# Conformer convolution in a two-layer trunk kernel: taps loaded and multiplied during the first FFN, second half of channels transformed in quarters, output projection by token tile

## The chip, the core and the metric

The kernel runs on one core of a Trainium2 chip. The metric is the device time of one execution, in microseconds. A core has five engines that run their own instruction queues: PE (TensorE, matrix products, with weight loads PEld), DVE (VectorE), ACT (ScalarE), POOL (GpSimd) and SP (SyncE, which here issues nearly all DMAs). They wait for each other through semaphores.

## What is computed

A backbone of two layers over 512 latent tokens of width 1024, with 256 context tokens; every sub-layer is wrapped in RMSNorm, a shift and scale from the conditioning vector, and a gated residual. Layer 0 mixes with a hybrid of gated DeltaNet heads and attention heads, layer 1 with a Conformer convolution; both end in a SwiGLU FFN. The change is in the Conformer:

```
def conformer_conv(h, w_in, b_in, dw_w, dw_b, ln_g, ln_b, w_out, b_out):
    val, gate = jnp.split(h @ w_in + b_in, 2, axis=-1)
    u = val * jax.nn.sigmoid(gate)
    u = depthwise_conv_centred(u, dw_w) + dw_b
    u = jax.nn.silu(layer_norm(u, ln_g, ln_b))
    return u @ w_out + b_out
```

`dw_w` has 31 taps for each of the 1024 channels. All data is fp32.

## The kernel before

**Products.** Each fp32 operand is split into a high part and a low part (a cast, then a subtraction), and each product is three matmuls: high by high, high by low, low by high. Weights come as 128x1024 tiles of 512 KB (`wraw`, L1700), are cast on ACT or DVE into `whi` (L564) and subtracted on DVE or POOL into `wlo` (L573). L564 and L573 are helpers for all casts and copies and all two-operand operations, so a group is told by its tiles.

**Order of work.** The program is written as operations with engines they may run on, a cost on each, what they depend on and which buffers they take and give back. The class `Plan` (from L62) sorts them: at every step it takes the operation with the earliest planned start, less a weight times the length of the work behind it and a bias from a table by the operation's name (`BIAS2`, L136, for this part). Buffers are counted as slots: 8 PSUM banks (`ps`), 46 slabs of 128x512 (`s`), 4 pairs of converted weights (`w`), 2 raw weight tiles (`wraw`), 2 window places (`win`). The result is a fixed order on every engine. `plan_tail` (from L1683) plans the last of four stretches: the output projection of the hybrid (phase 0), ffn(0) together with the dot products for later gates (phase 1), the Conformer (phase 2), ffn(1) (phase 3). The three stretches ahead of it are not touched.

**FFN.** For each pair of token tiles and each hidden slice, a gate bank and an up bank `ps_in` take 24 matmuls each (L204 to L206). ACT does silu from the gate bank (L1963), DVE multiplies with the up bank (L1966); only then are the banks free. The output projection (L1758 to L1760, `ps_y`) has two halves n of 512 columns and four token tiles t, a bank each. Each tile is squared and summed on ACT (L1779), multiplied by the gate row on DVE (`yg`, L1783), and added to the residual.

**Conformer.** The 1024 channels are worked in two halves n of 512. The input projection runs in four quarters q: n is q // 2, and each quarter brings 256 value and 256 gate columns for four token tiles (`ps_in`, L2105 to L2112). ACT takes the sigmoid of the gate (L2128), DVE multiplies (`csg`, L2131), and the result is split into `uh` and `ul`. The convolution is done by Fourier transform over the tokens. Three overlapping windows w cover two neighbouring token tiles each. `window(n, w)` makes real and imaginary parts with 12 matmuls into two banks `ps_ft` (L2166 to L2168), four products with the taps' spectra `specr` and `speci` on DVE (L2175), a sum and a difference, and two splits into `sph` and `spl`. `back(n, t)` transforms back into a bank `ps_y` (L2223 to L2229), one window for the outer token tiles, two for the inner ones. The bank is copied to `xtok` on ACT and its statistics are taken on DVE (`bs`, L2241). When both halves of a token tile are there, mean and variance are joined (L2266), POOL takes the root (L180), DVE normalises the two halves in place (`xtok`, L2278), PE transposes them (`ps_a`, L1830), ACT does silu with gain and bias (L2285), and the result is split into `ah` and `al` for the output projection, whose weights are `wcout`.

**The taps.** `ld_s` loads the taps in two halves (`taps`, L2065) and their 31 rows of cosines and sines (`tapf`, L2066), `s_mm` makes the spectra with four matmul groups into four banks `ps_sp` (L2076), and `s_put` copies these to `specr` and `speci`, which belong to buffers that open when ffn(0) has given up its own (`opened`).

## Time and profile before

| | us |
|---|---|
| median of 3 runs | 1390.94 (1390.02 to 1392.03) |
| the profiled execution | 1390.09 |
| its span | 1388.3 |
| PE busy | 1335.3 |
| DVE busy | 847.8 |
| ACT busy | 484.3 |
| POOL busy | 229.2 |

The profile is one execution; its times count from the start of the span. The page gives busy times, 40 slices with the clock that PE was granted, the chain of work that ended last, and groups of instructions by line, engine, operation and tile, with their mean time and what ended the idle time before them. Other views of the trace are the waits (which instruction waited for which engine's instruction, in total, how often, and the longest), the windows (busy time, count of instructions, clock and DMA share in a stretch) and the timeline. A matmul's own time overlaps that of its neighbours, so what one costs in a row of them is the stretch divided by their number.

### The profile page before, as it was taken

The numbers are of one execution on the slowest core, as the hardware profiler recorded it, in microseconds if no ns is written. First come the engines' busy times: TensorE is split into PE (matmuls) and PEld (weight loads), VectorE is DVE, ScalarE is ACT, GpSimd is POOL, SyncE is SP. The second block draws the span as 40 slices with busy tenths as digits, with TensorE's granted clock in tenths as the row PEclk, the third lists the DMA queues.
The fourth block names the chain that finished last, engine by engine and source line by source line (L and its number), as shares of the span: only waits on it lengthen the run. The fifth ranks groups of instructions, "written<-read, shape, count | busy, mean of one in ns | idle before, by whom it ended". The sixth has DMA issues, their size and how long they took to land.

```text
span 1388.3 us, 19096 instructions
## 1 busy us (share of the span) xinstructions
PE 1335.3 (96%) x7267; PEld 1121.0 (81%) x7267; DVE 847.8 (61%) x1631; ACT 484.3 (35%) x1019; POOL 229.2 (17%) x299
## 2 busy tenths in 40 slices
PE   6999998999999999999999899997999999999998
PEld 4888887889978988888888678885898888888886
DVE  3588897899877755656578454649464334343223
ACT  5656535776634211111100153214343222122221
POOL 2668562111002000000000210314040000000000
PEclk8999998999999999999999999998999999999999
DMA  8445635652265456455488413110213233233231
GB/s 313 139 131 172 149 121 117 208 160 89 65 198 196 145 160 197 153 165 182 163 269 270 160 48 105 61 46 31 76 62 122 78 104 103 79 122 106 91 101 66
DMA packets 105851, 184.74 MB, mean 133 GB/s; under 512 B 33731, under 2 KB 50450, under 8 KB 105760
## 3 DMA queue, kind: packets, MB, share of 16 engines
q1 hardware_dynamic: 105760, 183.53, 41.4%
q8 instruction: 57, 0.93, 0.3%
q14 instruction: 34, 0.28, 0.1%
HBM read 172.44 MB, written 11.06 MB: 132 GB/s over the span
## 4 chain that ended last, share of the span: by engine, by line
PE 82%; DVE 8%; DMA 4%; POOL 2%; ACT 2%; issue 1%; SPq 1%; DVEq 0%; POOLq 0%; ACTq 0%
PE ps_in L204 12%; PE ps_in L206 12%; PE ps_in L205 12%; PE ps_y L1758 7%; PE ps_y L1759 7%; PE ps_y L1760 7%; PE ps_in L2112 2%; PE ps_in L2110 2%; PE ps_in L2111 2%; PE ps_pt L1306 1%; PE ps_pv L1328 1%; PE ps_o L1369 1%; PE ps_sc L1276 1%; PE ps_du L1369 1%; PE ps_a L1830 1%
## 5 line engine op out<-in xcount | busy, mean ns | idle before, releaser
L206 PE MATMUL ps_in<-ah,wlo 128*128 128x512 f32 (+1 forms) x768 | 285.6, 372 | 1.1 <-DVE wlo L573 1.0
L204 PE MATMUL ps_in<-ah,whi 128*128 128x512 f32 (+1 forms) x768 | 285.7, 372 | 0.0
L205 PE MATMUL ps_in<-al,whi 128*128 128x512 f32 (+1 forms) x768 | 285.3, 371 | 0.0
L573 DVE TENSOR_TENSOR wlo<-wraw,whi 128x1024 fp32r<-128x1024 f32 x165 | 204.9, 1250 | 129.1 <-ACT whi L564 123.4
L206 PEld LDWEIGHTS ps_in<-ah,wlo 128*128 128x128 f32 x768 | 144.6, 188 | 26.7 <-DVE wlo L573 1.8
L204 PEld LDWEIGHTS ps_in<-ah,whi 128*128 128x128 f32 x768 | 144.7, 188 | 25.2 <-DVE whi L564 0.2
L205 PEld LDWEIGHTS ps_in<-al,whi 128*128 128x128 f32 x768 | 144.7, 188 | 24.9
L564 ACT CAST whi<-wraw 128x1024 fp32r<-128x1024 f32 x92 | 96.3, 1050 | 165.2 <-PE ps_y L1759 80.7
L1758 PE MATMUL ps_y<-whi,hh 128*128 128x512 f32 x352 | 138.9, 394 | 0.0
L1759 PE MATMUL ps_y<-whi,hl 128*128 128x512 f32 x352 | 138.4, 393 | 0.0
L1760 PE MATMUL ps_y<-wlo,hh 128*128 128x512 f32 x352 | 138.4, 393 | 0.0
L564 DVE CAST whi<-wraw 128x1024 fp32r<-128x1024 f32 x70 | 48.5, 693 | 140.7 <-PE ps_in L205 107.7
L1963 ACT ACTIVATE sg<-ps_in 128x512 f32<-128x512 f32 x44 | 26.3, 598 | 291.5 <-PE ps_in L206 291.2
L1625 DVE CUSTOM_DVE_ANT_0 wada<-wada,csrow 128x1024 f32<-128x1024 f32 x80 | 96.7, 1222 | 12.4 <-DMA wada<-in_wmB 12.0
L180 POOL TENSOR_TENSOR rr<-rr,mhalf 128x1 f32<-128x1 f32 x28 | 16.1, 576 | 489.5 <-DVE rr L1797 457.7
L1758 PEld LDWEIGHTS ps_y<-whi,hh 128*128 128x128 f32 x352 | 66.7, 189 | 15.9 <-issue 1.5
L1760 PEld LDWEIGHTS ps_y<-wlo,hh 128*128 128x128 f32 x352 | 66.6, 189 | 14.6
L1759 PEld LDWEIGHTS ps_y<-whi,hl 128*128 128x128 f32 x352 | 66.6, 189 | 14.4
L1966 DVE TENSOR_TENSOR sg<-sg,ps_in 128x512 f32<-128x512 f32 x44 | 30.0, 684 | 64.9 <-PE ps_in L206 64.9
L1779 ACT ACTIVATE junk<-ps_y 128x512 bf16<-128x512 f32 x32 | 19.1, 598 | 122.6 <-PE ps_y L1760 110.8
L573 POOL TENSOR_TENSOR matsl<-fraw,matsh 128x512 fp32r<-128x512 f32 x5 | 8.1, 1655 | 322.8 <-ACT matsh L564 322.8
L2110 PE MATMUL ps_in<-whi,ah 128*128 128x512 f32 x128 | 50.0, 391 | 0.0
(383 smaller groups left out, 2603.9 us busy)
## 6 DMA issues: line engine op xcount, KB each, us to landing
wraw<-in_wfin SPq DMA_DIRECT2D x88, 512.0 KB
wada<-in_wmB SPq DMA_DIRECT2D x80, 512.0 KB
wraw<-in_wfout SPq DMA_DIRECT2D x44, 512.0 KB
mraw<-in_wmA SPq DMA_DIRECT2D x16, 512.0 KB
wraw<-in_wcin SPq DMA_DIRECT2D x16, 512.0 KB
wraw<-in_wqkv SPq DMA_DIRECT2D x12, 512.0 KB
wraw<-in_wcout SPq DMA_DIRECT2D x8, 512.0 KB
rw<-grow SPq DMA_DIRECT2D x8, 384.0 KB
```

Source lines behind the costliest of these rows:

```text
L204: E.matmul(ps, wh, xh, start=start, stop=False)
L205: E.matmul(ps, wh, xl, start=False, stop=False)
L206: E.matmul(ps, wl, xh, start=False, stop=stop)
L564: {"ACT": S.copy, "DVE": V.tensor_copy, "Pool": G.tensor_copy}[e](dst, src)
L573: {"DVE": V, "Pool": G}[e].tensor_tensor(dst, a, b, o)
L1369: E.matmul(s[key][:m, h, 0:n], lhs(h), rhs(h), start=True, stop=True)
L1625: V.tensor_tensor_reduce(s["raw"], s["raw"], csrow[0], 1.0, 0.0, ALU.mult, ALU.add, accs[:, part, j : j + 1])
L1758: E.matmul(acc[t], ah[:, ts_], wh[:, o], start=i == 0 and j == 0, stop=False)
L1759: E.matmul(acc[t], al[:, ts_], wh[:, o], start=False, stop=False)
L1760: E.matmul(acc[t], ah[:, ts_], wl[:, o], start=False, stop=end)
L1966: V.tensor_tensor(s["g"], s["g"], pss[1]["ps"], ALU.mult)
L2110: E.matmul(acc[t], k["h"][:, tk], wh[:, o], start=False, stop=False)
```

## The change

Five edits, all in the tail or in the host's layout of the taps:

- The taps get a 32nd row of zeros, as do the cosines and sines; the three DMAs and the four matmul groups work on 32 rows. `ld_s` no longer depends on `opened`. `s_put` still does.
- The second half of channels is transformed in quarters of 256: `window_half(1, c, w)` takes the columns of quarter c alone, with 12 matmuls of 256 columns into one bank, which holds the real part in its left half and the imaginary part in its right. Its spectrum products are one of 512 and two of 256 columns, then one sum, one cast and one subtraction.
- `back(1, t)` runs in two passes of 256 columns into one bank.
- A window waits for the splits of its own quarter (`ops[c]`), where it waited for the last split of the half.
- The output projection of the Conformer takes its first half token tile by token tile, as the last four weight tiles of the second half already were (`bytile`).

The bias table `BIAS2` is new throughout. The diff, cut to its core:

```
-        def out_proj(lhs, src, part, ready, extra=None, free=None):
+        def out_proj(lhs, src, part, ready, extra=None, free=None, bytile=False):
...
-                by_i = np_ - 4 if n else np_
+                by_i = np_ - 4 if n or bytile else np_
...
-                    SP.dma_start(st["taps"][n][:31, :], I["cdw"][:, n * 512 : n * 512 + 512])
-                SP.dma_start(st["tapf"][:31, :256], I["ctap"])
-
-            ts_ = op({"SP": 3 * DMA}, ld_s, (opened,), lat=DLAT, take=("s", "s", "s"))
+                    SP.dma_start(st["taps"][n][:32, :], I["cdw"][:, n * 512 : n * 512 + 512])
+                SP.dma_start(st["tapf"][:32, :256], I["ctap"])
+
+            ts_ = op({"SP": 3 * DMA}, ld_s, lat=DLAT, take=("s", "s", "s"))
...
-                    ut["op"] = op({"DVE": 0.34, "Pool": 0.7}, c_low, (b,), rel=("s",))
+                    ut.setdefault("ops", []).append(op({"DVE": 0.34, "Pool": 0.7}, c_low, (b,), rel=("s",)))
...
+            def window_half(n, c, w):
...
+                def dft_q():
+                    s["ps"] = pbank("ps_ft")
+                    for i in range(2):
+                        o = s["ps"][:, i * 256 : i * 256 + 256]
+                        for j, (t, m) in enumerate(FWD[w]):
+                            mh, ml = mat(m + i)
+                            x = u[n][t]
+                            E.matmul(o, mh, x["h"][:, cc], start=j == 0, stop=False)
+                            E.matmul(o, mh, x["l"][:, cc], start=False, stop=False)
+                            E.matmul(o, ml, x["h"][:, cc], start=False, stop=j == 1)
...
+                def q_prod():
+                    s["x"] = slab("spa")
+                    V.tensor_tensor(s["x"].rearrange("p (i c) -> p i c", i=2), s["ps"].rearrange("p (i c) -> p i c", i=2),
+                                    bc(st["spec"][0][:, cs_], 1, (P, 2, 256)), ALU.mult)
...
+                def q_cross():
+                    s["y"] = slab("spb")
+                    V.tensor_tensor(s["y"][:, lo], s["ps"][:, hi], st["spec"][1][:, cs_], ALU.mult)
+                    V.scalar_tensor_tensor(s["y"][:, hi], s["ps"][:, lo], -1.0, st["spec"][1][:, cs_], op0=ALU.mult, op1=ALU.mult)
...
+                def q_comb():
+                    V.tensor_tensor(s["x"], s["x"], s["y"], ALU.add)
...
+                need = [u[n][t]["ops"][c] for t, _ in FWD[w]] + [mats[j] for j in range(2)]
...
+                for c in ((None,) if n == 0 else (0, 1)):
+                    cs_ = slice(0, 512) if c is None else slice(c * 256, c * 256 + 256)
...
+            for w in range(3):
+                window(0, w)
+            for w in range(3):
+                window_half(1, 0, w)
...
+            for t in range(NT):
+                back(0, t)
...
+            for w in range(3):
+                window_half(1, 1, w)
...
+            for t in range(NT):
+                back(1, t)
...
-            e = out_proj(lhs, I["wcout"], 6, ready, extra, free)
+            e = out_proj(lhs, I["wcout"], 6, ready, extra, free, True)
```

How the order moves, at three places. First SP's queue of DMAs, before, in ffn(0)'s output projection: `in_wfout` are its last weights, `in_wcin` the Conformer's first ones, `in_cmat` the transform matrices, `taps` and `tapf` the convolution's taps.

```order
L1700 DMA wraw<-in_wfout 128x1024
L2046 DMA fraw<-in_cmat 128x512 x5
L1700 DMA wraw<-in_wfout 128x1024
L2015 DMA bo<-in_cbias 8x512 x2
L1700 DMA wraw<-in_wcin 128x1024
L2065 DMA taps<-in_cdw 31x512 x2
L2066 DMA tapf<-in_ctap 31x256
L1700 DMA wraw<-in_wcin 128x1024
```

The same queue after, where the taps now stand, at the end of the hybrid's output projection: `in_wfin` are ffn(0)'s first weights, `in_wmB` the weights of the gates' dot products, `in_xs` the residual.

```order
L2390 DMA hres_5136<-in_xs 128x1024
L1622 DMA wada<-in_wmB 128x2x512 x3
L1700 DMA wraw<-in_wfin 128x1024 x4
L2065 DMA taps<-in_cdw 32x512 x2
L2066 DMA tapf<-in_ctap 32x256
L1622 DMA wada<-in_wmB 128x2x512 x4
```

The three transfers have moved from behind the first Conformer weight to a place ahead of nearly all of ffn(0)'s weights.

Second, PE before, in the second half of ffn(0)'s output projection (`ps_y`), around the four tap groups `ps_sp`:

```order
L1759 MATMUL ps_y<-whi,hl 128x512
L1760 MATMUL ps_y<-wlo,hh 128x512
L2076 MATMUL ps_sp<-taps,tapf 128x512 x4
L1758 MATMUL ps_y<-whi,hh 128x512
L1759 MATMUL ps_y<-whi,hl 128x512
```

PE after, in ffn(0)'s first hidden slices, which are worked 256 tokens wide:

```order
L206 MATMUL ps_in<-ah,wlo 128x256
L2076 MATMUL ps_sp<-taps,tapf 128x512
L204 MATMUL ps_in<-ah,whi 128x256
L205 MATMUL ps_in<-al,whi 128x256
L206 MATMUL ps_in<-ah,wlo 128x256
L204 MATMUL ps_in<-ah,whi 128x256
L205 MATMUL ps_in<-al,whi 128x256
L206 MATMUL ps_in<-ah,wlo 128x256
L2076 MATMUL ps_sp<-taps,tapf 128x512
```

The tap groups now stand one by one between ffn(0)'s matmuls, and nothing stands between the `ps_y` groups where they were.

Third, DVE before, where the last windows of the second half (`spa` to `spd`, `sph`, `spl`) meet the first normalisations (L2278):

```order
L564 CAST sph<-spa 128x512
L573 TENSOR_TENSOR spl<-spa,sph 128x512
L564 CAST sph<-spb 128x512
L573 TENSOR_TENSOR spl<-spb,sph 128x512
L2175 TENSOR_TENSOR spa<-ps_ft,specr 128x512
L2175 TENSOR_TENSOR spc<-ps_ft,speci 128x512
L2175 TENSOR_TENSOR spd<-ps_ft,speci 128x512
L2175 TENSOR_TENSOR spb<-ps_ft,specr 128x512
L2278 TENSOR_SCALAR xtok<-xtok,mv 128x512 x2
L564 CAST sph<-spa 128x512
L573 TENSOR_TENSOR spl<-spa,sph 128x512
```

DVE after, at its first normalisations (now L2348), with `csg` and `uh` of the last input tile between them:

```order
L573 TENSOR_TENSOR spl<-spa,sph 128x512
L2301 BN_STATS bs<-ps_y 128x6
L2336 BN_AGGR mv<-bs 128x2
L2337 TENSOR_SCALAR mv<-mv 128x1
L2348 TENSOR_SCALAR xtok<-xtok,mv 128x512 x2
L2131 TENSOR_TENSOR csg<-ps_in,csg 128x256
L564 CAST uh<-csg 128x256
L2348 TENSOR_SCALAR xtok<-xtok,mv 128x512 x2
L573 TENSOR_TENSOR wlo<-wraw,whi 128x1024
```

The four full-width products ahead of the first normalisation and the two splits behind it have gone; one quarter of the last window (`spa`, `spb` from L2237 on) stands after both pairs of normalisations.

More of the change, by code (lines that the diff above doesn't have):

```diff
@@ L2075, in s_mm @@
                         w["ps"] = pbank("ps_sp")
-                        E.matmul(w["ps"], st["tapf"][:31, i * P : i * P + P], st["taps"][n][:31, :], start=True, stop=True)
+                        E.matmul(w["ps"], st["tapf"][:32, i * P : i * P + P], st["taps"][n][:32, :], start=True, stop=True)
                     def s_put(e, n=n, i=i, w=w):
@@ L2197, in sp_lo @@
                     return f
-                need = [u[n][t]["op"] for t, _ in FWD[w]] + [mats[j] for j in range(2)]
+                need = [o for t, _ in FWD[w] for o in u[n][t]["ops"]] + [mats[j] for j in range(2)]
                 r = op({"PE": 1.36}, dft(0), need, take=("ps", "win"))
@@ L2215, in window, with q_hi, q_lo @@
                 s["used"] = []
[L2217 to L2233 removed]
+            def window_half(n, c, w):
+                s = ab[n, c, w] = {}
+                cc, cs_ = slice(c * 256, c * 256 + 256), slice(n * 512 + c * 256, n * 512 + c * 256 + 256)
+                lo, hi = slice(0, 256), slice(256, 512)
+                def dft_q():
[18 more added lines that the diff above has]
+                    V.tensor_tensor(s["x"], s["x"], s["y"], ALU.add)
+                def q_hi(e):
+                    s["h"] = slab("sph", F32R)
+                    copy_on(e, s["h"], s["x"])
+                def q_lo(e):
+                    s["l"] = slab("spl", F32R)
+                    tt_on(e, s["l"], s["x"], f32(s["h"]), ALU.subtract)
+                need = [u[n][t]["ops"][c] for t, _ in FWD[w]] + [mats[j] for j in range(2)]
+                r = op({"PE": 1.44}, dft_q, need, take=("ps",))
+                for t, _ in FWD[w]:
+                    uu[n, t].append(r)
+                p = op({"DVE": 0.62}, q_prod, [r] + specs[n], take=("s",) * 4)
+                y = op({"DVE": 0.68}, q_cross, [r] + specs[n], seq=(p,))
+                op({}, None, (p, y), rel=("ps",))
+                x = op({"DVE": 0.6}, q_comb, (p, y), rel=("s",))
+                z = op({"ACT": 0.5, "DVE": 0.34}, q_hi, (x,))
+                s["ops"] = [op({"DVE": 0.6, "Pool": 1.23}, q_lo, (z,), rel=("s",))]
+                s["used"] = []
@@ L2241, in c_stat @@
                     V.bn_stats(st["bs"][:, t, n, :], s["ps"])
-                b = op({"ACT": 0.55, "DVE": 0.6}, c_tok, o, take=("s",))
+                b = op({"ACT": 0.55, "DVE": 0.6}, c_tok, allo, take=("s",))
                 c = op({"DVE": 0.6}, c_stat, (o[0], b))
@@ L2462, in _layout @@
                                  a(conf_b_out)[0].reshape(2, 512)], 0)
[L2463 removed]
+    A["cdw"] = np.concatenate([a(conf_dw_w)[0], np.zeros((1, D), np.float32)])
     A["clnp"] = np.stack([a(conf_ln_g)[0].reshape(KT, P).T, a(conf_ln_b)[0].reshape(KT, P).T], -1)
```

62 lines of the change are left out of this document (35 added, 27 removed).

## The prediction

> **What bounds the kernel now.** I read the page first, for the engine that fills the span. The rows under the busy times are 40 equal slices of 34.7 us.
>
> ```profile
> span 1388.3 us, 19096 instructions
> PE 1335.3 (96%) x7267; PEld 1121.0 (81%) x7267; DVE 847.8 (61%) x1631; ACT 484.3 (35%) x1019; POOL 229.2 (17%) x299
> PE   6999998999999999999999899997999999999998
> ```
>
> PE is 96% busy, so only two things can make this kernel shorter: PE slices below 9, and matmuls at a slow clock. Behind the start there are two low places, slice 23 (from 763 us, with the hole at 790) and slice 28 (about 950). The second view is the waits of PE from 440 us to the end, by the instruction that waits and its releaser: total, times, longest.
>
> ```profile
> PE ps_a L1830 <- DVE xtok L2278: 8.9, 5, 2.7
> PE ps_sp L2076 <- DMA tapf<-in_ctap: 5.2, 1, 5.2
> PE ps_in L206 <- DVE wlo L573: 1.0, 2, 0.8
> PE ps_a L1830 <- DVE xm L570: 0.7, 1, 0.7
> PE ps_y L2228 <- DVE spl L573: 0.2, 1, 0.2
> ```
>
> That is all: 14.1 us in the waits for the taps' DMA and for the normalised tokens, and 1.9 elsewhere. The third view is the windows: busy time and instructions of PE, PEld, DVE, ACT, POOL, then PE's granted clock, the share of the 16 DMA engines, GB/s.
>
> ```profile
> 450.00:750.00 300.00, 299.67 (x1396) 250.99 (x1396) 193.79 (x280) 45.25 (x73) 0.76 (x2) 1.00 0.57 186
> 789.00:806.00 17.00, 11.82 (x21) 6.27 (x22) 1.29 (x2) 2.34 (x4) 0.00 (x0) 0.60 0.15 53
> 792.00:794.00 2.00, 0.00 (x0) 0.00 (x0) 0.00 (x0) 0.00 (x0) 0.00 (x0) 0.50 0.07 24
> 801.00:805.00 4.00, 4.00 (x10) 2.96 (x10) 0.00 (x0) 0.58 (x1) 0.00 (x0) 0.50 0.00 0
> 900.00:930.00 30.00, 30.00 (x133) 24.53 (x132) 11.92 (x21) 5.65 (x9) 4.38 (x6) 1.00 0.11 36
> 930.00:945.70 15.70, 15.70 (x70) 12.77 (x68) 15.34 (x24) 3.55 (x5) 7.97 (x7) 1.00 0.10 34
> 945.70:972.40 26.70, 17.49 (x70) 13.17 (x70) 25.32 (x51) 14.40 (x30) 9.71 (x8) 0.81 0.12 40
> 972.40:1000.00 27.60, 27.60 (x123) 22.85 (x122) 10.84 (x16) 7.64 (x15) 0.34 (x1) 1.00 0.29 96
> 1030.00:1040.00 10.00, 10.00 (x86) 10.00 (x85) 3.43 (x7) 2.37 (x6) 3.77 (x6) 1.00 0.09 36
> ```
>
> At full clock a 512-wide matmul costs 27.60/123 = 0.224 us, a 256-wide one (the last row, in the second FFN) 10/86 = 0.116. ffn(0), 450 to 750, is full to 0.3 us.
>
> **Hole one, 789 to 806.** The chain of waits names it:
>
> ```profile
> 784.81 9.23 DMA tapf<-in_ctap
> 794.18 6.31 PE ps_sp L2076 x7
> ```
>
> The taps are 31-row transfers behind a 512 KB weight; at 792 to 794 the DMA share is 0.07, one engine of 16, with 24 GB/s. PE stands from 789.0 to 794.2, then runs the 8 tap matmuls at a clock of 0.50 (0.90 us each), then ps_y at 0.40 us a matmul until about 806. In these 17 us PE does 8 tap matmuls and 12 or 13 of ps_y, worth 13 x 0.224 = 2.9. So the place costs 14.1 us beyond ps_y's work.
>
> **Hole two, 945.7 to 972.4.** The PE groups there (mean ns of one behind the busy time):
>
> ```profile
> L1830 PE MATMUL ps_a<-masks,xtok 128*128 128x128 f32 x32 | 5.7, 319 | 8.9 <-DVE xtok L2278 8.9
> 961.28 1.11 PE L1830 MATMUL ps_a<-masks,xtok 128*128 128x128 f32 x8 [1.66 <-DVE xtok L2278]
> ```
>
> It is 32 transposes and 38 matmuls: 38 x 0.224 = 8.5, and the transposes 4.4 (the last row, of the timeline, has eight in 1.11), together 12.9 of 26.7 us. The hole costs 13.8. From 930 to 945.7 DVE is busy 15.34 of 15.7, then 25.32 of 26.7; from 900 to 930 only 11.92 of 30. So DVE is the bound for some 40 us and had 18 us free just before. Its chain there:
>
> ```profile
> 937.24 1.45 DVE sph L564
> 939.83 0.35 DVE sph L564
> 949.84 2.51 DVE xtok L2278 x2
> 952.39 1.12 PE ps_a L1830 x4
> 961.75 4.97 DVE xtok L2278 x2
> ```
>
> The same cast takes 0.35 or 1.45, the same pair of normalisations 2.51 or 4.97. The timeline and the tile's minimum say when:
>
> ```profile
> L2278 DVE TENSOR_SCALAR xtok<-xtok,mv x8: 531/856/2564, 949.8 to 964.2; 128x512 f32<-128x512 f32 x8
> 960.69 6.03 DVE L2278 TENSOR_SCALAR xtok<-xtok,mv 128x512 f32<-128x512 f32 x4
> 961.60 4.83 POOL L573 TENSOR_TENSOR wlo<-wraw,whi 128x1024 fp32r<-128x1024 f32 x2
> ```
>
> Alone one is 0.53 us; four beside two POOL subtractions took 6.03. On the chain this adds about 1.1 for each of some four casts, 1.45 and 3.9 for the pairs: 9.7 us.
>
> **The change, part by part.** The sum is made against the profiled execution, 1390.1 us (span 1388.3 and 1.8 around it); the median of three runs is 1390.9, within 0.1%.
>
> *Taps early.* The three DMAs now stand at the head of ffn(0)'s weights, long before they were, and the tap matmuls inside ffn(0)'s first weights; where they stood, ps_y runs on. Hole one goes: -14.1. The 8 tap matmuls are paid at full clock, half of 0.90 each: +3.6 (at least 8 x 0.224 = 1.8). Net -10.5, between -12.3 and -10. The three transfers pass SP's ada weights, whose readers are covered in ffn(0) by a DVE that is 35% free; I cost them at nothing, at most the 0.8 us that one weight wait of the list costs. What is next at that place is the Conformer's first weights and h tokens: DVE and ACT stood idle there behind the taps (the row at 792) and lose that rest. Following the new order with the durations of the trace, the narrowest place keeps about 0.6 us; I put +0.5, between 0 and 5.2 (a wait as long as the old one).
>
> *Four banks held.* The spectra are still put away only once the Conformer's buffers open, so the tap matmuls hold 4 of the 8 PSUM banks through ffn(0) and into the second half of its output projection. The rows that decide:
>
> ```profile
> L1963 ACT ACTIVATE sg<-ps_in 128x512 f32<-128x512 f32 x44 | 26.3, 598 | 291.5 <-PE ps_in L206 291.2
> L1966 DVE TENSOR_TENSOR sg<-sg,ps_in 128x512 f32<-128x512 f32 x44 | 30.0, 684 | 64.9 <-PE ps_in L206 64.9
> L1783 DVE TENSOR_TENSOR yg<-ps_y,gm 128x512 f32<-128x512 f32 x32 | 21.8, 685 | 7.9 <-ACT junk L1779 7.9
> L573 DVE TENSOR_TENSOR wlo<-wraw,whi 128x1024 fp32r<-128x1024 f32 x165 | 204.9, 1250 | 129.1 <-ACT whi L564 123.4
> L564 DVE CAST whi<-wraw 128x1024 fp32r<-128x1024 f32 x70 | 48.5, 693 | 140.7 <-PE ps_in L205 107.7
> ```
>
> A bank comes free 0.60 us (silu) or 0.60 + 0.68 (and the product) after its last matmul. In the new order 24 matmuls of a bank freed earlier (24 x 0.224 = 5.4 us) cover that at each turn, and at the output projection's turn each of four banks needs a yg (0.68) with two pairs of casts and subtractions (1.9 a pair) between: 6.8 us against 8.2 of matmuls. Cost 0; without the cover 1.3 per turn.
>
> *Quarters.* A window of the second half costs DVE four products, two casts, two subtractions, in three windows behind the last input tiles:
>
> ```profile
> L2175 DVE TENSOR_TENSOR spa<-ps_ft,specr 128x512 f32<-128x512 f32 x3 | 2.1, 686 | 0.1
> L573 DVE TENSOR_TENSOR spl<-spb,sph 128x512 fp32r<-128x512 f32 x4 | 2.8, 692 | 0.1
> L2131 DVE TENSOR_TENSOR csg<-ps_in,csg 128x256 f32<-128x256 f32 x1 | 0.4, 414 | 0.0
> ```
>
> That is 4 x 0.68 + 2 x 0.35 + 2 x 0.69 = 4.8, or 14.4 for the three. A quarter costs one product 0.69, two crosses at 256 (csg's 0.41 each), a sum and a subtraction at 0.69: 2.9, its cast on ACT. The first three quarters need input tile q=2 alone and fall in the free 18 us; of the second three, one stands behind the first transposes. So 2 x 2.9 = 5.8 is left of 14.4 in the chain: 8.6 us shorter. If all slowing beside POOL stayed, 13.8 - 8.6 = 5.2 of the hole would remain; if it all went (9.7), none. The sums of this half leave POOL, but one 2.4 us subtraction and the ul's still stand beside the first normalisations, so I leave 3.0: -10.8, between -13.8 and -8.6. How a rest of waits is paid is disputed. The rows have it: at 952 a wait of 2.7 is followed by matmuls of 0.43 us in the chain after 952.39, so a short wait also halves the clock for some 3 us, 1.5 us more.
>
> ```profile
> 953.51 0.43 PE ps_y L2227
> 953.94 0.43 PE ps_y L2228
> ```
>
> The Trainium skill, "TensorE: Matmul & The Clock Gate", section "HAM oscillation — how this bites in real kernels", puts the loss of clock at idle gaps above about 3.4 us; this row disagrees, with 2.7 us and shorter gaps in a row. By that rule the rest would be 1.5 and the sum 1.5 us lower.
>
> The narrower matmuls: 152 of 0.116 for 76 of 0.224 is 17.6 for 17.0, +0.6.
>
> *Output projection by token tile.* All four weight pairs of the first half are now used by every tile, so the second half's pairs come free only during tile 3 (25 x 0.224 = 5.6 us). Its DVE chain is three whi (0.69), four wlo (1.25) and a yg that waits for the tile's end: the last is ready about 11 us after the tile's start, needed at 10.3. +1.0, between 0 and 3.8 (two whole conversions).
>
> **Sum:** 1390.1 - 10.5 + 0.5 - 10.8 + 0.6 + 1.0 = 1370.9.
>
> **Rivals.** *The normalisations stay late.* DVE is again the bound, hole two only moves: 1390.1 - 10.5 + 0.5 + 0.6 + 1.0 = 1381.7, or 1373.1 with 5.2 us left. For it: the order still has POOL's wlo near. Against: the 18 free us. Chance 0.15.
>
> *Something else stands at 790.* A first Conformer weight waits in place of the taps: 5.2 and its half clock, some 8: 1378. The wait rows name no weight there, but the taps may have hidden one. Chance 0.10.
>
> *Both holes close whole* and the projection's weights are in time: 1370.9 - 3.0 - 0.5 - 1.0 - 1.8 = 1364.6. Chance 0.10.
>
> *Slower: four banks starve ffn(0).* If the products on DVE fall behind the weights (194/300 of a turn of 96 x 0.224 = 21.5 us is 13.9 of DVE work), every turn of two tile pairs waits 1.3 for each pair: 2 x 1.3 x 10 turns = 26, which gives 1396.9. It decides from 0.96 per wait, where 20 of them eat the whole gain of 19.2. Against it: DVE at 194 of 300 us. By the Trainium skill, "TensorE: Matmul & The Clock Gate", section "A second HAM failure mode: psum-queue depth-cycling", short idles between groups that cycle through banks also lose clock; no row of ffn(0) shows it, and it would add to this price. Chance 0.06.
>
> **How the numbers follow.** The forecast has 0.59, as the sum of terms with one likely value each: 1366 to 1375. The range 1364 to 1381 takes in the whole closing, the wait at 790 and most of the late normalisations. About 0.2%, 2.8 us, is what a measurement of this kernel tells from no change. Only the bank case is slower (0.06); mishaps that would cancel the gain to within 2.8 us get 0.02; faster 0.92.
>
> **What would show it.** Right: no wait of ps_sp for tapf; clock 1.00 at the place before the Conformer; ps_in without waits in ffn(0); waits of ps_a for xtok of some 1 to 3 us in all, and one of about 1 us for wlo in the middle of the Conformer's projection. Wrong: waits of ps_in for sg in ffn(0), xtok waits above 5 us, or a DVE still solid for 40 us ahead of the transposes.

## The result, and the profile after

The changed kernel takes 1381.67 us (median of 4 runs, 1379.68 to 1382.74); the kernel before takes 1391.47 beside it (4 runs, 1390.02 to 1392.03). The ratio is 0.9929, with an interval of 0.9912 to 0.9947: faster by 0.7%, about half of the gain that was forecast (1370.9), and just outside the range (to 1381). The profiled execution took 1380.72. The ratios below leave out three far slower executions, of 1950 to 2784 us (one of before, two of e3_junction).

First the page, after: the span, the busy times, and PE's busy share and granted clock in slices of 34.5 us.

```profile
span 1378.9 us, 19257 instructions
PE 1330.0 (96%) x7343; PEld 1118.7 (81%) x7343; DVE 859.7 (62%) x1650; ACT 460.8 (33%) x996; POOL 242.9 (18%) x309
PE   5989998999999999999999999999999999999998
PEclk8999998899999999999999999999999999999999
```

From the tenth slice on every digit is a 9 in both rows, but for the last of PE. The low places at 790 and 950 are gone; the granted clock is 1.00 at both. The waits of PE from 440 us on say the same (total, times, longest):

```profile
PE ps_a L1830 <- DVE xm L570: 1.9, 2, 1.7
PE ps_in L205 <- POOL al L573: 1.6, 2, 1.0
PE ps_y L2284 <- DVE spl L573: 1.4, 1, 1.4
PE ps_y L1758 <- DVE ah L564: 1.2, 1, 1.2
PE ps_y L1758 <- DVE yg L1783: 0.7, 1, 0.7
PE ps_y L1760 <- DVE wlo L573: 0.7, 2, 0.4
PE ps_in L206 <- DVE rr L1874: 0.6, 1, 0.6
PE ps_in L206 <- DVE wlo L573: 0.4, 2, 0.2
PE ps_a L1830 <- DVE xtok L2348: 0.3, 1, 0.3
```

The 5.2 us for tapf are gone and the 8.9 for xtok are 0.3. Beside them stand eight small waits, 8.5 us together, where before had 1.9. So both holes closed, and 10 us of the forecast are still missing. The next step is to cut the span into stages at matmuls that both kernels have, and to take each stage's length from the timeline. All times are starts of the first matmul of the stage:

| stage | begins before | begins after | change of its length | forecast |
|---|---|---|---|---|
| up to the first `mixd` matmul of the hybrid projection | 0 | 0 | +0.77 | 0 |
| A: from there to ffn(0)'s 512-wide matmuls | 407.80 | 408.57 | +8.98 | +3.6 (tap matmuls) |
| B: ffn(0) up to its output projection | 469.37 | 479.12 | +0.52 | 0 (held banks) |
| C: output projection (hole one) | 687.00 | 697.27 | -13.29 | -14.1 |
| D: Conformer, to the first matmul on tokens 2 and 3 | 824.01 | 820.99 | +1.98 | +0.5 |
| E: from there to the end (hole two, the Conformer's output projection, second FFN) | 837.14 | 836.10 | -8.32 | -10.8 + 0.6 + 1.0 |
| the last matmul ends | 1381.98 | 1372.62 | -9.36 in all | -19.2 |

Stage E isn't cut at the Conformer's output projection, since that matmul has other company now: it starts 11.2 us earlier than before against the stage's start, but 16 transposes (8 take 1.11) and 13 narrow matmuls (0.116 each), 3.7 us together, stand behind it that stood ahead of it before. Where the order is the same in two kernels, a length repeats closely: the distance from the stage's start to that projection is 11.18 to 11.20 us shorter than before in after and ten of the kernels below. Apart from the tap matmuls, and from the narrower matmuls in E, each stage has the same matmuls in every kernel here, only in another order. So stages can be compared between single profiles, as long as no clock change falls into them and no transfer comes late (e2 below shows both).

Stage A is where the gain went. PE's timeline of after (start, duration, in brackets the wait) shows two losses in it:

```profile
449.00 0.39 PE L205 MATMUL ps_in<-al,whi 128*128 128x256 f32 x1 [0.51 <-POOL al L573]
451.81 0.39 PE L205 MATMUL ps_in<-al,whi 128*128 128x256 f32 x1 [1.04 <-POOL al L573]
...
462.73 1.12 PE L2076 MATMUL ps_sp<-taps,tapf 32*128 32x512 f32 x2
465.41 1.12 PE L2076 MATMUL ps_sp<-taps,tapf 32*128 32x512 f32 x2
```

and POOL's timeline there the cause of the waits:

```profile
443.80 7.96 POOL L573 TENSOR_TENSOR al<-a,ah 128x256 fp32r<-128x256 f32 x6
```

The new numbers put all sixteen subtractions `al` of ffn(0)'s tokens on POOL, six of them in 7.96 us, and PE waits for them. Before, DVE made twelve of the sixteen, in pairs of 0.75. The second loss is the tap matmuls, which come behind that, one pair at a time. Before, DVE was busy for 45.94 of the stage's 61.60 us and POOL for 10.35. The window (busy PE, PEld, DVE, ACT, POOL, clock, DMA share, GB/s):

```profile
407.80:469.40 61.60, 60.71 (x370) 53.68 (x369) 45.94 (x93) 24.37 (x49) 10.35 (x12) 1.00 0.49 168
```

Hole two, in the windows of after:

```profile
930.00:943.00 13.00, 11.50 (x64) 9.56 (x63) 12.93 (x17) 4.94 (x7) 8.45 (x5) 1.00 0.24 81
943.00:955.30 12.30, 10.67 (x77) 9.46 (x75) 12.13 (x23) 8.43 (x14) 6.57 (x5) 1.00 0.05 7
```

From 930 to the start of the output projection, at 955.3, DVE is solid for 25 us; before, the projection started at 967.5, after 35.8 busy us of 37.5. What POOL slows has changed as well. Rows of DVE in after:

```profile
934.46 2.78 DVE L573 TENSOR_TENSOR spl<-spa,sph 128x512 fp32r<-128x512 f32 x1
937.17 2.87 DVE L573 TENSOR_TENSOR spl<-spb,sph 128x512 fp32r<-128x512 f32 x1
...
941.82 0.68 DVE L573 TENSOR_TENSOR spl<-spa,sph 128x512 fp32r<-128x512 f32 x1
...
948.76 1.00 DVE L2348 TENSOR_SCALAR xtok<-xtok,mv 128x512 f32<-128x512 f32 x2
950.33 1.40 DVE L2348 TENSOR_SCALAR xtok<-xtok,mv 128x512 f32<-128x512 f32 x2
```

and of POOL:

```profile
934.16 2.53 POOL L573 TENSOR_TENSOR wlo<-wraw,whi 128x1024 fp32r<-128x1024 f32 x1 [0.77 <-ACT whi L564]
936.95 2.53 POOL L573 TENSOR_TENSOR wlo<-wraw,whi 128x1024 fp32r<-128x1024 f32 x1 [0.25 <-ACT whi L564]
```

Two subtractions that take 0.68 alone take 2.8 beside POOL's: each ends about 0.55 us after POOL's does. But now that happens ahead of the normalisations; the pairs of normalisations that took 2.51 and 4.97 take 1.00 and 1.40.

### The profile page after: what moved, and what is told of

It is laid out like the page before. It is cut to its first block, busy times and chain, and to the rows that moved or that the text cites. A ratio compares the mean times of both kernels' runs of the same rounds, so it can differ in the third digit from the quotient of the medians.

```text
span 1378.9 us, 19257 instructions
## 1 busy us (share of the span) xinstructions
PE 1330.0 (96%) x7343; PEld 1118.7 (81%) x7343; DVE 859.7 (62%) x1650; ACT 460.8 (33%) x996; POOL 242.9 (18%) x309
## 4 chain that ended last, share of the span: by engine, by line
PE 75%; DVE 10%; DMA 6%; POOL 3%; issue 3%; ACT 2%; SPq 0%; DVEq 0%; POOLq 0%; ACTq 0%
PE ps_in L204 12%; PE ps_in L206 12%; PE ps_in L205 12%; PE ps_y L1758 6%; PE ps_y L1760 6%; PE ps_y L1759 6%; DMA wada<-in_wmB 2%; PE ps_in L2110 2%; PE ps_in L2112 2%; PE ps_in L2111 2%; DVE wlo L573 2%; PE ps_pt L1306 1%; DVE wada L1625 1%; PE ps_pv L1328 1%; PE ps_o L1369 1%
## 5 line engine op out<-in xcount | busy, mean ns | idle before, releaser
L564 DVE CAST whi<-wraw 128x1024 fp32r<-128x1024 f32 x93 | 64.8, 697 | 158.5 <-PE ps_in L205 109.4
L564 ACT CAST whi<-wraw 128x1024 fp32r<-128x1024 f32 x69 | 72.2, 1049 | 121.7 <-PE ps_y L1759 70.5
L1625 DVE CUSTOM_DVE_ANT_0 wada<-wada,csrow 128x1024 f32<-128x1024 f32 x80 | 97.4, 1232 | 18.3 <-DMA wada<-in_wmB 18.1
L1779 ACT ACTIVATE junk<-ps_y 128x512 bf16<-128x512 f32 x32 | 19.1, 598 | 138.0 <-PE ps_y L1760 121.6
L653 DVE SCALAR_TENSOR_TENSOR cv<-ps_in,convw,cv 128x510 f32<-128x510 f32 (+3 forms) x80 | 49.1, 636 | 1.6 <-ACT cv L568 0.2
```

The costliest lines, as they stand in the source:

```text
L564: {"ACT": S.copy, "DVE": V.tensor_copy, "Pool": G.tensor_copy}[e](dst, src)
L653: V.scalar_tensor_tensor(s["cv"][:, o], s["ps"][:, i], convw[:, ft, j : j + 1], s["cv"][:, o], op0=ALU.mult, op1=ALU.add)
L1625: V.tensor_tensor_reduce(s["raw"], s["raw"], csrow[0], 1.0, 0.0, ALU.mult, ALU.add, accs[:, part, j : j + 1])
```

## The experiments

The kernel before ran beside every group of kernels, on the same chip, at a median of 1392.0 to 1394.0 us (1391.5 beside after). So ratios are compared, not times. The stages are those of the table above, as changes against before, from one profile of each kernel; the kernels are told in the order in which they ran. The stretch ahead of A, which no edit touches, is 0.4 to 5.6 us longer than before in these profiles, so their stages do not add up to the ratios.

| kernel | A | B | C | D | E | ratio to before | interval |
|---|---|---|---|---|---|---|---|
| after | +9.0 | +0.5 | -13.3 | +2.0 | -8.3 | 0.9929 | 0.9912 to 0.9947 |
| e1_rows32 | 0.0 | 0.0 | -8.6 | 0.0 | +0.4 | 0.9930 | 0.9908 to 0.9952 |
| e2_al_dve | +6.5 | +0.4 | -8.0 | +2.0 | -7.3 | 0.9924 | 0.9901 to 0.9947 |
| e3_junction | +24.2 | +0.5 | -13.4 | +2.0 | -8.3 | 1.0029 | 1.0013 to 1.0045 |
| e4_order01 | +13.6 | 0.0 | -9.0 | +3.7 | -8.3 | 0.9984 | 0.9970 to 0.9999 |
| e5_late_order01 | 0.0 | 0.0 | -9.8 | +4.8 | -8.4 | 0.9887 | 0.9870 to 0.9904 |
| e6_late | +5.1 | 0.0 | -9.0 | +2.0 | -8.3 | 0.9894 | 0.9878 to 0.9909 |
| e7_mid | 0.0 | +3.7 | -9.2 | +4.8 | -8.5 | 0.9908 | 0.9894 to 0.9923 |
| e8_full_width | +8.8 | +1.3 | -13.3 | +2.0 | +4.9 | 1.0010 | 0.9996 to 1.0024 |
| e9_start_dve | 0.0 | 0.0 | -7.3 | +1.6 | -8.0 | 0.9869 | 0.9850 to 0.9887 |
| e10_no_bytile | +0.1 | 0.0 | -7.3 | +4.4 | +2.1 | 0.9962 | 0.9947 to 0.9977 |
| e11_both | +0.1 | 0.0 | -10.5 | +1.6 | +3.7 | 0.9959 | 0.9943 to 0.9974 |
| e12_31rows | +19.1 | +0.6 | -13.1 | +2.0 | -7.8 | one run: 1393.9 us |  |
| e13_spread | +0.1 | 0.0 | -9.3 | +1.6 | -8.5 | 0.9886 | 0.9869 to 0.9902 |
| e14_late_al_dve | +1.4 | 0.0 | -8.9 | +2.0 | -8.0 | 0.9911 | 0.9895 to 0.9926 |

**e1_rows32: the row count alone, in the kernel before.**

```diff
-                    SP.dma_start(st["taps"][n][:31, :], I["cdw"][:, n * 512 : n * 512 + 512])
-                SP.dma_start(st["tapf"][:31, :256], I["ctap"])
+                    SP.dma_start(st["taps"][n][:32, :], I["cdw"][:, n * 512 : n * 512 + 512])
+                SP.dma_start(st["tapf"][:32, :256], I["ctap"])
...
-                        E.matmul(w["ps"], st["tapf"][:31, i * P : i * P + P], st["taps"][n][:31, :], start=True, stop=True)
+                        E.matmul(w["ps"], st["tapf"][:32, i * P : i * P + P], st["taps"][n][:32, :], start=True, stop=True)
```

> The kernel before with one edit: the taps are moved as 32 rows in place of 31 (the last row zero); the order is that of before, and the transfers still wait for the Conformer's buffers. Theory A (the row count made the transfer slow, since one DMA engine of 16 carried it at 24 GB/s): PE's wait for tapf falls from 5.2 us to under 1, the low clock behind it shortens, and the time is 5 to 11 us below before, 1380 to 1386. Theory B (the place in SP's queue, behind a 512 KB weight, made it late, and only the earlier issue closes the hole): 4 us or more of that wait stay and the time is within 3 us of before.

Theory A. The transfer is issued where it was, and PE hardly waits for it. The SP queue and PE in the timeline of this kernel:

```profile
788.57 0.41 SPq L2066 DMA_DIRECT2D tapf<-in_ctap  x1
```

```profile
792.38 3.94 PE L2076 MATMUL ps_sp<-taps,tapf 32*128 32x512 f32 x8 [0.24 <-DMA tapf<-in_ctap]
```

From issue to the first tap matmul it is 3.8 us; before it was 9.4 (784.81 to 794.18). Stage C is 8.6 shorter, and the kernel's order is that of before on every engine. One row of zeros brings as much as the whole change (0.9930 against 0.9929).

**e2_al_dve: after, with al on DVE.**

```diff
-                    b = op({"DVE": 0.68, "Pool": 1.37}, p_low, (b,), rel=("s",))
+                    b = op({"DVE": 0.68, "Pool": 1.37} if ph[0] == "3" else {"DVE": 0.68}, p_low, (b,), rel=("s",))
```

> The kernel after, with the subtractions al of the FFN's and the Conformer's h on DVE in place of POOL, as most of them were before. Theory A (POOL's al is one part of what ffn(0)'s start lost): the waits of ps_in for POOL al (1.6 us) go, the stage from ffn(0)'s first matmul to its 512-wide ones shortens by 1.5 to 3 us, and the time is 1378 to 1380.5. Theory B (DVE, which converts the weights there, becomes late instead): waits for wlo or ah grow by as much, and the time is within 1 us of after (1381.7) or above.

Theory A as far as ffn(0)'s start goes: stage A is 2.5 shorter than in after. But in this profile stage C gives 5.3 back, and the time (1382.6, theory B's) is not told apart from after's. What does it is a longer wait (0.7 in after) at the turn into the output projection's second half, with a clock of 0.50 behind it:

```profile
PE ps_y L1758 <- DVE yg L1783: 3.6, 1, 3.6
```

```profile
760.00:764.00 4.00, 3.46 (x8) 2.79 (x9) 3.90 (x6) 0.00 (x0) 0.00 (x0) 0.50 0.30 116
```

Three `yg` stand one behind the other there, while the tap matmuls hold four of the eight banks. The edit is not the cause: from ffn(0)'s output projection on, every engine has the order of after. What differs is one of the dot products for later gates (L1625) that DVE makes ahead of the `yg`. Its wait for its weights, in e2 and in after:

```profile
750.21 1.22 DVE L1625 CUSTOM_DVE_ANT_0 wada<-wada,csrow 128x1024 f32<-128x1024 f32 x1 [3.01 <-DMA wada<-in_wmB]
748.25 1.22 DVE L1625 CUSTOM_DVE_ANT_0 wada<-wada,csrow 128x1024 f32<-128x1024 f32 x1 [1.24 <-DMA wada<-in_wmB]
```

Against the stage's start that is 2.9 us later in e2 (53.9 and 51.0), and the `yg` and PE are as much later. The forecast had the cover (8.2 us of matmuls for 6.8 of DVE) and priced its loss at 1.3 per turn; it left the dot products and their transfers out. The profiled execution is the slowest of the six (1386.15; the fastest took 1377.76), so how often this happens is not known, nor why the transfer came late.

**e3_junction and e4_order01: other orders of the same early taps.** e3 takes the scheduler's numbers for the first output projection from before, e4 also those for ffn(0). Some of the entries:

```diff
-'ld_w0': -2762, 'w_high0': 22720, 'w_low0': -17249, 'reopen0': -102230,
+'ld_w0': -7542, 'w_high0': 3066, 'w_low0': -6231, 'reopen0': -48619,
...
```

> The kernel after, with the scheduler's numbers for the first output projection's weights as before. Only the stretch from that projection to ffn(0)'s first matmuls is ordered anew: the tap matmuls stand in the output projection of the hybrid part, in one group of 4 times two passes, and not one by one between ffn(0)'s first weights. Theory A (the order of this stretch lost 9 us: the tap matmuls 4.2, waits behind POOL's al and the weights the rest): the shift of the 512-wide ffn(0) matmuls against before falls from +9.8 to about +5 or less, and the time is 1375 to 1379. Theory B (the early taps themselves, their transfers and held banks, cost it wherever they stand): the shift at the 512-wide matmuls stays at +8 to +11 and the time within 1.5 us of after.

> The kernel after, with the scheduler's numbers for the first output projection and for the whole of ffn(0) as before; the Conformer and the second FFN keep those of after. Theory A (as in the run beside it, the numbers' order of the junction is the loss): the shift at the 512-wide ffn(0) matmuls is +2 to +5, that at the Conformer's first matmul -9 to -11, and the time 1372 to 1378. Theory B (early taps cost it in any order): the shift is +8 or more there and the time 1380 or more.

Neither theory's numbers hold for e3: stage A grew by 24.2, not by 5 or 9, and the kernel is slower than before. In e4 it grew by 13.6, which is theory B. In both the tap matmuls stand close together in the hybrid output projection, and stage A has a low clock that after does not have: a mean of 0.86 in e3 and 0.91 in e4, with PE idle for 9.9 and 4.2 us (after: 1.00 and 3.8). So the old order does not help as long as the taps are early; whether the order or the early taps are at fault could not be said from these two.

**e5_late_order01 and e6_late: the taps wait for the Conformer's buffers again,** in e4's order and in after's:

```diff
-            ts_ = op({"SP": 3 * DMA}, ld_s, lat=DLAT, take=("s", "s", "s"))
+            ts_ = op({"SP": 3 * DMA}, ld_s, (opened,), lat=DLAT, take=("s", "s", "s"))
```

> The kernel of the run e4_order01 (32 rows, quarters, projection by tile, first stages by the old numbers) with one thing undone: the taps' transfers wait for the Conformer's buffers again, as before. Up to ffn(0)'s output projection its order is that of before. Theory A (early taps are what spoils ffn(0)'s start, whose transfers and tap matmuls push the weights back; 32 rows alone close most of hole one): from the first output projection to ffn(0)'s 512-wide matmuls it takes no longer than before (within 0.5 us), the stage to the Conformer's first matmul is 8 to 9 us shorter than before as in e1_rows32, the normalisations' place 11.4 shorter, and the time is 1372 to 1377. Theory B (the order of those stages cost it, not the early taps): no change against e4_order01, 1389 to 1393.

> The kernel after with one thing undone: the taps' transfers wait for the Conformer's buffers again; the scheduler's numbers are all those of after. Theory A (early taps spoil ffn(0)'s start): its two stages (+2.2 and +6.8 in after) fall to under +3 together, the stage to the Conformer's first matmul is 8 to 9 shorter than before, and the time is 1374 to 1379. Theory B (the new numbers' order, al on POOL above all, cost it): the two stages still lose 5 us or more, and the time is 1381 to 1386, above after.

e5 goes to theory A (the time, 1377.3, is 0.3 above what it expected). In e6 the stages are theory B's and the time, 1379.1, is nearly theory A's. Both have a part: with the taps late, stage A costs 0.0 in the old order and 5.1 in the new one; with the taps early, 13.6 and 9.0. So of after's 9.0, 5.1 stay when the taps are late, and 3.9 go with the early taps. The two causes do not simply add: in the old order the early taps cost 13.6, and with early taps the new order is the better one by 4.6. And early issue, taken by itself in after's order, is worth nothing: stages A, B and C add up to -3.8 in after (+9.0 + 0.5 - 13.3) and to -3.9 in e6_late (+5.1 - 9.0). Both late kernels are faster than after: 0.9887 and 0.9894 against 0.9929, the intervals apart.

**e7_mid: early taps, but late in ffn(0).** The numbers for `ld_s` and `s_mm` are those of before as well:

```diff
-'ld_s2': -19945, 's_mm2': 32209, 's_put2': 45330,
+'ld_s2': -6553, 's_mm2': -2183, 's_put2': -19037,
```

> The kernel of e4_order01 with the scheduler's numbers for the taps as before too: they are still not held back for the Conformer's buffers, but the tap matmuls stand late in ffn(0), some 390 PE rows ahead of where before had them, in a stretch without waits. Theory A (the taps' bad place is ffn(0)'s start, and only that): the start takes as long as before, the tap matmuls cost 1.8 to 4 us in ffn(0), the stage to the Conformer's first matmul is about 13 shorter, so 9 to 11 us net at hole one, and the time is 1371 to 1376. Theory B (four held banks slow ffn(0) wherever the taps stand): ffn(0)'s second half loses 5 us or more, and the time is 1378 or more.

Between the two, with theory B's time (1380.7). The start costs nothing and the tap matmuls 3.7, as in theory A, but stage C is 9.2 shorter and not 13, because PE waits 3.9 at the projection's turn, where the held banks leave little cover:

```profile
PE ps_y L1758 <- DVE yg L1783: 3.9, 2, 2.3
```

It is slower than e5_late_order01 by the medians, with intervals that overlap (0.9894 to 0.9923 and 0.9870 to 0.9904). None of the early places tried (after, e3, e4, e7) is better than the late ones; here what the start saves is lost again at the turn.

**e8_full_width: after without quarters.**

```diff
-                for c in ((None,) if n == 0 else (0, 1)):
+                for c in (None,):
...
-            for w in range(3):
-                window_half(1, 0, w)
...
+                for w in range(3):
+                    window(n, w)
```

> The kernel after with the second half of the channels transformed at full width again, not in quarters; the taps and the projection as in after. Theory A (the quarters alone close hole two): 8 to 11 us are lost again between the first normalisation's transposes and the output projection, the waits of ps_a for xtok are back at 6 us or more, and the time is 1389 to 1393. Theory B (the new order of the Conformer, with POOL's weight subtractions away from the normalisations, closed it): less than 4 us are lost there and the time is 1382 to 1386.

Theory A, and more than that (1394.8 us, where it expected up to 1393): stage E is 13.2 us longer than in after. The wait is back:

```profile
PE ps_a L1830 <- DVE xtok L2338: 7.7, 2, 7.4
```

The numbers of the order were made for quarters, so 13.2 is the price of taking them out here; against before, which never had them, the stage gained 8.3.

**e9_start_dve, e10_no_bytile, e11_both: the two smaller losses,** on e5_late_order01. e9 gives the first quarter's weights to DVE alone, e10 takes the by-tile projection out, e11 has both:

```diff
-                ws = [weights(I["wcin"][q, i]) for i in range(4)]
+                ws = [weights(I["wcin"][q, i], onv=q == 0) for i in range(4)]
```

```diff
-            e = out_proj(lhs, I["wcout"], 6, ready, extra, free, True)
+            e = out_proj(lhs, I["wcout"], 6, ready, extra, free)
```

> The kernel of the run e5_late_order01 with one instruction moved: the one weight subtraction wlo that POOL does at the Conformer's start (2.73 us there) goes to DVE, one place later. Theory A (DVE's casts ah beside that POOL subtraction take 2.64 us a pair in place of 0.49, and PE's wait of 2.5 us for ah is theirs): the pair falls to about 0.5, the wait goes, the stage from the Conformer's first matmul to its tokens 2 and 3, which was 4.8 us longer than before, shortens by 2 to 4 us, and the time is 1373.5 to 1375.5. Theory B (DVE has no room for 1.2 us more there): the stage stays as long within 1 us, the wait only changes its name, and the time is 1376.5 to 1378.5.

> The kernel of the run e5_late_order01 with the Conformer's output projection in the order of before (all weights over all token tiles, not the last four by tile). Theory A (projecting by token tile costs a wait for the weights, +1.0 in the forecast, and is part of the +3.1 measured between the projection's start and the second FFN): that stage shortens by 1 to 3 us and the time is 1374 to 1376.5. Theory B (the by-tile order pays: without it the second FFN's first tokens come late): the stage lengthens by 1 us or more and the time is 1378.5 to 1382.

> Both edits of the two runs beside it together on e5_late_order01. If they are independent, the gain is the sum of theirs: 1371 to 1375 if both pay; it is the version to be compared with before and after.

e9: theory A for the stage. Only one instruction moves from POOL to DVE, and stage D falls from +4.8 to +1.6. The same slow casts are in after too, in two rows at its Conformer's start, of DVE and of POOL:

```profile
824.28 2.70 DVE L564 CAST ah<-a 128x256 fp32r<-128x256 f32 x2
```

```profile
824.06 2.56 POOL L573 TENSOR_TENSOR wlo<-wraw,whi 128x1024 fp32r<-128x1024 f32 x1
```

and the same cast in e9, with POOL idle:

```profile
823.52 0.49 DVE L564 CAST ah<-a 128x256 fp32r<-128x256 f32 x2
```

It is the mechanism of hole two at another place. In after the wait at that place has another name (1.7 us of `ps_a` for `xm`, which DVE makes behind these casts), and the edit was not tried there; and stage D is still 1.6 longer than before in e9. The time is 1375.85 (just above what theory A expected), with a ratio of 0.9869; whether it is faster than e5_late_order01 the intervals leave open, since stage C of this profile came out 2.5 longer (below). It has the lowest ratio of the kernels here, and it beats after (0.9912 to 0.9947) and before.

e10 goes to theory B, and far beyond (1389.5 us, where it expected up to 1382): stage E lengthens by 10.5 against e5_late_order01. Its waits:

```profile
PE ps_y L2283 <- ACT sph L564: 3.4, 1, 3.4
PE ps_a L1830 <- DVE xtok L2348: 2.8, 2, 2.4
PE ps_y L2284 <- DVE spl L573: 2.6, 2, 2.3
```

They stand in the inverse transforms and the normalisations, not at the output projection's weights. Without the by-tile edit the same numbers place the inverse transforms elsewhere among the input projection's matmuls, so what is measured is the by-tile order with all that follows from it. That the by-tile form itself pays is not shown by this; that taking it out of this order costs 10 us is. e11 has both effects, a loss and a gain: E near that of e10, D as in e9, and a time of 1388.0.

**e12_31rows: after with 31 rows.** The diff is that of e1_rows32 the other way round.

> The kernel after with the taps moved as 31 rows again, nothing else. Theory A (issued early, the slow transfer is hidden, so that the row count no longer matters): no wait of PE for tapf over 0.5 us, the stage to the 512-wide ffn(0) matmuls and that to the Conformer's first matmul as in after within 0.5 us. Theory B (its slow transfer still delays the tap matmuls or the weights queued behind it): a wait of 1 us or more for tapf, or for wlo or wada, at ffn(0)'s start, and that stage longer by as much.

Theory B. Stage A is 10.2 us longer than in after. PE's timeline and its windows:

```profile
467.63 2.04 PE L2076 MATMUL ps_sp<-taps,tapf 31*128 31x512 f32 x2 [3.21 <-ACT ah L564]
```

```profile
467.60:484.00 16.40, 16.37 (x43) 9.71 (x44) 5.36 (x10) 1.52 (x2) 1.53 (x3) 0.50 0.52 159
```

The row names ACT as the releaser, but after has the same instructions in the same order and waits for nothing there; the one thing that differs is the transfer. It was issued at 457.6 and takes as long as before had it, some 10 us. Behind the wait of 3.2 the clock is 0.50 for 16 us, in which PE stands only 0.03 us. So the row count counts at both places: 8.6 us late, 10.2 early, each in one profile.

**e13_spread: the tap matmuls of e9 set apart.** A dependence on the copy before, with a planned latency, puts six matmuls of `ps_y` between one pair and the next; nothing else moves on PE.

```diff
-                    b = op({"PE": 0.86}, s_mm, (ts_,), take=("ps",))
+                    b = op({"PE": 0.86}, s_mm, (ts_,) + put, take=("ps",))
...
-                    specs[n].append(op({"ACT": 0.5, "DVE": 0.6}, s_put, (b, opened), rel=("ps",)))
+                    specs[n].append(op({"ACT": 0.5, "DVE": 0.6}, s_put, (b, opened), rel=("ps",), lat=7.0)); put = (specs[n][-1],)
```

> The kernel of the run e9_start_dve with its four groups of two tap matmuls set apart, six matmuls of ffn(0)'s output projection between one and the next; the order of every other instruction is the same. Theory A (eight 32-row matmuls in a row, 3.7 us, let the clock fall in some executions): the clock is 1.00 at that place, the stage to the Conformer's first matmul is 9.5 to 11 us shorter than before, the runs spread less, and the time is 1372.5 to 1375. Theory B (the fall has to do with something else at that place, the wait for the transfers or the weights' DMA): the clock falls in this profile too, or the stage and the spread of the runs are as in the runs without it, and the time is 1375 to 1378.

The clock is as theory A has it, the time is not. The windows of e9 over and behind its eight tap matmuls (785.5 to 790.0), and those of e13:

```profile
785.50:787.50 2.00, 2.00 (x6) 1.01 (x6) 1.90 (x3) 1.04 (x2) 0.00 (x0) 1.00 0.03 8
787.50:789.50 2.00, 2.00 (x4) 0.47 (x3) 1.30 (x2) 1.17 (x2) 0.00 (x0) 0.69 0.45 86
789.50:793.50 4.00, 4.00 (x9) 2.82 (x9) 0.00 (x0) 1.10 (x2) 0.00 (x0) 0.50 0.61 219
```

```profile
783.90:787.90 4.00, 4.00 (x12) 1.91 (x12) 2.28 (x2) 0.81 (x2) 0.00 (x0) 1.00 0.41 132
787.90:792.50 4.60, 4.60 (x16) 2.39 (x14) 0.73 (x2) 0.95 (x2) 0.00 (x0) 1.00 0.42 140
```

Stage C is -9.3 here, in place of -7.3 in e9 with its low clock, but e5 and e11, whose eight stand in a row and kept the clock, have -9.8 and -10.5. The five runs spread less (1374.4 to 1378.1, against 1371.3 to 1379.8 for e9), but the ratios are not told apart (0.9886 and 0.9869, on different chips, with intervals that overlap). By the stages, setting them apart trades the chance of a low clock (about 2 to 3 us here) for a cost of half to one.

**e14_late_al_dve: e6_late with al on DVE** (the edit of e2).

> The kernel of the run e6_late (after with the taps waiting for the Conformer's buffers) with the subtractions al of the FFN's h on DVE in place of POOL, as in e2_al_dve. Theory A (POOL's al is what the new order lost at ffn(0)'s start): its two stages, +2.6 and +2.5 against before in e6_late, fall to under +2 together, and the time is 1374 to 1377. Theory B (the order of the weights and the residual's additions lost it): they stay at +4 or more and the time is within 1 us of e6_late's 1379.

Theory A for the stage: +5.1 falls to +1.4, so 3.7 of the 5.1 that the new order costs with late taps go when DVE makes `al` (with early taps, in e2, it was 2.5). The time doesn't show it, and is theory B's (1379.0): 0.9911 against 0.9894, with overlapping intervals, on different chips. What the runs gain or lose outside the profiled one, the profile can't say.

## Why the prediction was half right

Summed over stages the profile has -9.4 us where the forecast had -19.2:

- *Hole one and the tap matmuls.* Forecast -14.1 and +3.6, measured -13.3 and +3.9. Right in size, but for the wrong one of two edits: "Taps early" was given the whole of it. The profile had the other reason in hand (one DMA engine of 16, 24 GB/s, at 792 to 794), and the forecast named it without asking what the 32 rows would do alone. They do as much alone (-8.6 in e1_rows32, -9.8 in e5_late_order01); issuing early gains nothing (stages A to C: -3.8 in after, -3.9 in e6_late), since the tap matmuls cost at ffn(0)'s start what they no longer cost later.
- *The step that failed* is the price of the place to which the taps were moved. The sum charges it with the tap matmuls and puts all else there at nothing: "The three transfers pass SP's ada weights, whose readers are covered in ffn(0) by a DVE that is 35% free; I cost them at nothing". Those 35% are ffn(0)'s middle, from 450 to 750. In stage A before, DVE was 25% free (the row above). The transfers did not cost much (3.9 with the matmuls, forecast 3.6). But the new numbers reorder everything from the hybrid projection to ffn(0)'s first weights as well, and the sum had no term for that. It is +5.1 with the taps late (e6_late), of which 3.7 go when DVE makes al (e14_late_al_dve); the other 1.4 stay open. This is half of the missing 9.8; the rest is 1.5 at the Conformer's start, 1.1 at hole one and the tap matmuls, 0.9 in stage E, 0.5 in B and 0.8 ahead of the stages, where the change touches nothing.
- *Four banks held.* Forecast 0, measured +0.5 in B and one wait of 0.7 in C. The worry was at the right place: the same wait is 3.6 in e2, in after's own order, and 3.9 in e7, so the cover at the projection's turn is thin. The forecast's 6.8 us of DVE work there (its terms, 4 x 0.68 and 2 x 1.9, give 6.5) lack the dot products, of 1.22 each, and their waits for transfers; that after lost only 0.7 is in part luck. The slower rival, a starved ffn(0), did not come: B is +0.5.
- *Conformer start.* Forecast +0.5 within 0 to 5.2, measured +2.0. One pair of casts on DVE runs beside one subtraction on POOL (2.70 for 0.49). That this makes PE wait is shown by e9 in e5's order; in after it is read from the rows, where PE waits 1.7 for `xm` behind these casts.
- *Hole two and the projection by tile.* Forecast -10.2 (with the narrower matmuls) and +1.0, measured -8.3 together. The mechanism held: the quarters shorten DVE's chain, and the slowing beside POOL moves ahead of the normalisations; taken out again they cost 13.2 (e8). One step of it did not: the first three quarters were to fall into DVE's free 18 us before 930, but only one has its product there (at 916.9; the next two start at 929.5 and 932.2), and DVE is busy for 10.8 us from 900 to 930, no more than before (11.9). What is left are the waits for spl (1.4), ah (1.2) and wlo (0.4 and 0.3, in the projection, as forecast in kind). That the by-tile edit costs 1.0 was argued from its own wait for weights; e10 shows that it can't be judged so, because the inverse transforms' places hang on it. "Something else stands at 790" and "the normalisations stay late" did not come; that the second one's 1381.7 is the measured time is a coincidence. Of the signs that the forecast named for being wrong none came, and of those for being right "ps_in without waits in ffn(0)" failed, in stage A (1.6 for al).

The clock behind a wait was halved in hole one of before and behind the 3.2 us in e12. The forecast's rest of 3.0 at hole two was 1.5 us of waits and 1.5 for a halved clock behind them. The clock was not paid: after's waits there (1.4, 0.3 and 1.2, together 2.9) pass with a granted clock of 1.00 from 930 to 970. So this term came out right by two errors that cancel, which is luck. In other profiles somewhat longer waits go both ways: a wait of 2.25 for spl was followed by 0.50 for 3.4 us in e11 (939.0 to 942.4), and the same wait in e10 by 1.00. The Trainium skill, "TensorE: Matmul & The Clock Gate", section "Part 1: The HAM clock gate (the "warmup" mystery)", has the monitor's window at 3.4 us and free-running, so that the same work may or may not be caught. That agrees with this pair, and with the tap matmuls: eight in a row take 3.7 us (e5: 783.18, x8), and the clock fell behind them in e1, e3, e6, e9, e10 and e14, and stayed at 1.00 in e5, e7 and e11.

## What to carry to other kernels

When a change brings two edits for one wait, ask of the rows which of them the wait needs: here a transfer on one engine of 16 was the cause, and a row of zeros was enough. Work that is moved out of a hole is paid where it lands; price that place by its own rows (here the start of a stage, where weights, tokens and splits all come at once), not by the stage's mean, and if a table of numbers is new throughout, give each stretch that it reorders a term of its own. Then look at which engine gets each short operation: here a subtraction on POOL cost twice, by its own length and by what DVE did beside it.

## What was not expected of the hardware

- **Row count.** A transfer of 31 rows takes 9.4 us from issue to use, one of 32 rows 3.8 (before and e1_rows32, same place in the queue).
- **Clock without a wait.** Eight tap matmuls of 32 rows in a row, with PE busy throughout, were followed by a granted clock of 0.50 in six of the nine kernels that had them so: for 3.4 us in e1, e6 and e14, for 6.8 in e3, e9 and e10 (added up from windows). That is once or twice the 3.4 us window that the Trainium skill's page named above has. Stage C has the same order on every engine in e5, e9, e10 and e11, and the clock fell in two of the four. In the four profiles with two at a time among other matmuls (after, e2, e8, e13) it stayed at 1.00. The cost is half of that time, 1.7 or 3.4 us. Thirteen profiles make the link likely, not certain, and why 32 rows should count for less was not tried.
- **DVE beside POOL.** Casts of 128x256 took 2.70 a pair beside a POOL subtraction and 0.49 without, subtractions of 128x512 2.8 and 0.68, while a spectrum product, which reads PSUM, kept its 0.67 (the rows of DVE and of POOL in after). The Trainium skill, "GPSIMD Engine Reference", section "1. Specifications", says that the two engines contend for SBUF, with VectorE instructions in a two-port mode or with two inputs from there. The rows agree for the subtractions, with two such inputs, and for the product, with one; of the casts, with one, they show the slowing and not the mode.

```profile
943.63 0.67 DVE L2237 TENSOR_TENSOR spa<-ps_ft,specr 128x512 f32<-128x512 f32 x1
944.22 0.41 DVE L2242 TENSOR_TENSOR spb<-ps_ft,speci 128x256 f32<-128x256 f32 x1
```

```profile
943.89 1.30 POOL L573 TENSOR_TENSOR spl<-spa,sph 128x512 fp32r<-128x512 f32 x1 [4.42 <-ACT sph L564]
```

The product and the cross of 256 columns stand beside POOL's subtraction at their usual lengths.
